# Layer 1's modulation vectors computed wholly on VectorE, in three places of a two-layer diffusion backbone

## The chip, the cores and the metric

The kernel runs on one core of a Trainium2 chip. What counts is the device time of one execution in microseconds; lower is better. The kernel before took 1163.95, 1163.52 and 1162.24 us in three runs, a median of 1163.52 us.

## The reference

Two layers, each a token-mixing part and a feed-forward part, for 256 latent tokens (modulated by `c`) and 128 context tokens (modulated by `c_ctx`), 1024 wide. Cut to what matters here:

```python
def layer(x, mod, p, latent, kc, vc):
    sh1, sc1, g1, sh2, sc2, g2 = split(mod, 6)        # six vectors of 1024
    h = layer_norm(x) * (1 + sc1) + sh1               # group A: sh1, sc1
    z = h @ p["w_in"] + p["b_in"]
    ... attention, depthwise convolution, Fourier mixing, three gated projections -> merged
    x = layer_norm(ALPHA * x + g1 * (merged @ p["w_o"]), p["ln1_g"], p["ln1_b"])   # group G: g1
    h = layer_norm(x) * (1 + sc2) + sh2               # group B: sh2, sc2
    u = dwconv3(h @ p["w_up"], ...)
    ug, uv = split(u, 2)
    x = layer_norm(ALPHA * x + g2 * ((silu(ug) * uv) @ p["w_down"]), p["ln2_g"], p["ln2_b"])  # G: g2

for l in range(2):
    mod_ctx = silu(c_ctx) @ w_mod[l] + b_mod[l]       # w_mod[l]: 1024 x 6144
    mod_lat = silu(c) @ w_mod[l] + b_mod[l]
    ...
```

So each layer needs six vectors of 1024 for each of two conditions: groups A (shift and scale ahead of the mixing), G (the gate of the mixing, index 0, and that of the feed-forward part, index 1) and B (shift and scale ahead of the feed-forward part).

## The kernel before

All weights are fp32. A product is made of three matmuls (`mm3`, L196 to L198): weight and activation are each split in a high part (`whi`, cast by ScalarE, L179) and the rest (`wlo`, a subtraction on VectorE, L180). Weights come in 1 MB tiles (`raw`, 128x2048), all loaded by `load` (L121), nearly all of them from SyncE's queue. A scheduler puts the instructions of each engine in a fixed order ahead of time; at run time each engine (and SyncE's queue of DMA issues) works its list strictly in that order, and an instruction that waits holds all behind it.

The modulation vectors are made in three ways:

- Group A of layer 0, at the start, on TensorE (`mod_first`).
- G and B of layer 0, and G and B of layer 1, on TensorE, each in the mixing part of its own layer: `mod_stream` loads `w_mod` in 256 KB pieces, eight to a step, and each step issues eight small fp32 matmuls (L217, `acc<-s,cpad`; the trace shows them as 16 records). There are eight steps to a layer. The last step of G ends in `mod_gates` (a memset on GpSimd at L268, four bias loads, an addition, four writes to the DRAM scratch `gscr`), the last of B in `mod_columns` (a copy out of PSUM on VectorE, L282; four transposes on TensorE, L286; four additions, L294).
- Group A of layer 1, on VectorE, in layer 0's feed-forward loop: `mod_rows` takes `w_modr`, the same weights stored the other way, in 512 KB tiles of 128x1024; each tile is multiplied with the broadcast rows of silu(c) and silu(c_ctx) and summed along the row (L315, SCALAR_TENSOR_TENSOR with `accum_out`, two to a tile). There are 16 tiles, hence 32 such instructions. The two broadcast rows come from the DRAM scratch `cscr`, which the setup writes at L154.

The gates are read back from `gscr` by `gate_bc`, each row broadcast to 128 partitions (512 KB a read), just ahead of the `close` that uses them: L817 multiplies the PSUM result by the gate, L818 adds the residual, L820 and L824 apply the layer norm's scale `lg` and bias `lb`, which `ln` loads bring.

In the mixing part the attention's scores and softmax come first, mixed with the taps of the depthwise convolution (L785, VectorE); then branches 1 and 2, whose products are gated on VectorE (L562) and added up on GpSimd (L563, `g<-g,g`). In the feed-forward part a loop over u = 0 to 10 makes two pairs of up-projection tiles (taps of the small convolution on ScalarE L927 and VectorE L928, L930; the gating L946 to L951) and one piece of the down projection.

Of the kernel before, what the change touches and what calls it, by code (L numbers as in the profile page):

```python
# [16 lines left out]
P = 128  # L17
D = 1024
# [59 lines left out]
class Net:  # L78
# [3 lines left out]
    def __init__(self, ctx, tc, a):  # L82
        self.tc, self.nc, self.a = tc, tc.nc, a
        self.sb = ctx.enter_context(tc.tile_pool(name="sb", bufs=1))
        self.ps = ctx.enter_context(tc.tile_pool(name="ps", bufs=1, space=bass.MemoryType.PSUM))
        self.dr = ctx.enter_context(tc.tile_pool(name="dr", bufs=1, space=bass.MemoryType.DRAM))
        self.n = 0
        self.modcol, self.bmod, self.colsets = {}, {}, {}


    def t(self, tag, shape, dtype=F32):
# [39 lines left out]
    def setup(self):  # L131
        nc, a = self.nc, self.a
        self.zeros = self.const("zeros", [P, P])
        nc.vector.memset(self.zeros, 0.0)
        self.busy(self.WARM)
        self.ident = self.const("ident", [P, P])
        make_identity(nc, self.ident)
        self.mhalf = self.const("mhalf", [P, 1])
        nc.gpsimd.memset(self.mhalf, -0.5)
        self.zero2 = self.const("zero2", [P, 2 * KD])  # L140
        nc.gpsimd.memset(self.zero2, 0.0)
        self.cpad = self.const("cpad", [P, KD, 32])
        nc.gpsimd.memset(self.cpad, 0.0)
        ct, ch = self.kk()[0:2 * KD, :], self.kk()[0:2 * KD, :]
        self.load(ct, a["c2"])
        nc.vector.tensor_scalar(ch, ct, 0.5, None, op0=ALU.mult)
        nc.scalar.activation(ct, ch, AF.Tanh)
        nc.vector.scalar_tensor_tensor(ch, ct, 1.0, ch, op0=ALU.add, op1=ALU.mult)
        pt = self.psum()
        nc.tensor.transpose(pt[:, 0:2 * KD], ch, self.ident[0:2 * KD, 0:2 * KD])  # L150
        nc.vector.tensor_copy(
            self.cpad[:, :, 0:2], pt[:, 0:2 * KD].rearrange("p (v k) -> p k v", v=2))
        self.cscr = self.dr.tile([2, D], F32, tag="cscr", name="cscr", bufs=1)
        nc.sync.dma_start(self.cscr.rearrange("v (k p) -> (v k) p", p=P), ch)  # L154
        self.gscr = self.dr.tile([DEPTH, 2, 2, D], F32, tag="gscr", name="gscr", bufs=1)
        self.xscr = self.dr.tile([3, P, D], F32, tag="xscr", name="xscr", bufs=1)

    def setup_late(self):
        nc, a = self.nc, self.a
        att = self.const("att", [P, 128 + 768])  # L160
        self.load(att, a["k_att"])
        self.rope = att[:, 0:128].rearrange("p (t s c) -> p t s c", t=2, s=2)
        self.mask = att[:, 128:896].rearrange("p (t k) -> p t k", t=2)
        self.kT = [[self.sb.tile([P, 512], F32R, tag=f"kT{v}{i}", name=f"kT{v}{i}", bufs=1) for i in range(2)]
                   for v in range(NKV)]
        self.upad = [self.const(f"upad{i}", [P, UP_W]) for i in range(2)]
        for u in self.upad:
            nc.gpsimd.memset(u, 0.0)
# [124 lines left out]
                dst = self.modcol[l][:, gi, v, ks].rearrange("p (i q) -> p i q", q=ns)  # L293
                nc.vector.tensor_tensor(dst, part, bias, op=ALU.add)  # L294

    def mod_rows(self, l, kind):

        nc, a = self.nc, self.a
        cb = [self.bcast(self.cscr[v]) for v in range(2)]
        prod = self.s4()  # L300
        w = [self.s4() for _ in range(2)]
        b0 = 3 if kind == "B" else 0
        tiles = [(j, k) for j in range(2) for k in range(KD)]
        sums = [self.sm(16) for _ in range(2)]

        def fetch(n):
            j, k = tiles[n]
            self.load(w[n % 2], a["w_modr"][l - 1, self.MODS[kind], j, k])

        fetch(0)  # L310
        fetch(1)
        yield
        for n, (j, k) in enumerate(tiles):
            for v in range(2):
                nc.vector.scalar_tensor_tensor(prod, w[n % 2], 1.0, cb[v], op0=ALU.mult, op1=ALU.mult,  # L315
                                               accum_out=sums[j][:, v * KD + k:v * KD + k + 1])
            if n + 2 < len(tiles):
                fetch(n + 2)
            if k == KD - 1:
                for v in range(2):  # L320
                    nc.vector.tensor_tensor(self.modcol[l][:, j + (2 if kind == "B" else 0), v, :],
                                            sums[j][:, v * KD:(v + 1) * KD], self.bmod[l][:, j + b0, :], op=ALU.add)
            yield

    def gate_bc(self, l, j):
        out = []
# [179 lines left out]
        self.b_out(l, 1, acc, z, bb)  # L506


    def mixing(self, l, first, hT, mods):
        nc, a = self.nc, self.a  # L510
        z = [self.s4() for _ in range(3)]
        (self.start_first if l == 0 else self.start_next)(l, first, hT, z)
# [57 lines left out]

        if l + 1 < DEPTH:
            self.columns(l + 1)
        mods = self.mod_stream(mods)

        def mod():
            next(mods, None)

        ci = conv_in()
        next(ci)
        cv = self.keys(l, z)  # L580
# [20 lines left out]
                mod()  # L601
        for i, _ in enumerate(branch(1, 0, "w_a", 4, aT, lambda: values(3))):
            next(cb, None)
            if i % 2:
                mod()
        for i, _ in enumerate(branch(2, 1, "w_c", 2, cT, lambda: [None for _ in cb])):
            if i % 2:
                mod()
        for _ in mods:
            pass  # L610
        return m_hl

    def fourier(self, f, out):
# [228 lines left out]
    TAIL = 5  # L842
    NF = 4

    def layer(self, l, first, hT, mods):
        nc, a = self.nc, self.a
        m_hl = self.mixing(l, first, hT, mods)
        gate = self.gate_bc(l, 0)
        lg, lb = self.bcast(a["ln"][l, 0]), self.bcast(a["ln"][l, 1])
        acc = [[self.psum("acc"), self.psum("acc")] for _ in range(3)]  # L850
# [53 lines left out]
            for q in range(2):  # L904
                self.split_hT(t, 4 * q, 4, h2f[t][q], h2, GAP)

        rows = self.mod_rows(l + 1, "A") if l + 1 < DEPTH else iter(())
        gT = {}
        off2 = (0, P, 2 * P + GAP)
        held = []  # L910
# [23 lines left out]
        for u in range(KF // 2):  # L934
            ws = []
            for v in range(2):
                if 2 * u + v * KF in pre:
                    ws.append([None, None])
                else:
                    ws.append(self.halves(self.col_halves(self.raw(a["w_u"][l, u, v]))))  # L940
            for h in range(2):
                i = 2 * u + h
                cg = up_tile(i, ws[0][h])
                th = self.g()
                nc.scalar.activation(th, cg, AF.Tanh)  # L945
                nc.vector.scalar_tensor_tensor(cg, th, 1.0, cg, op0=ALU.add, op1=ALU.mult)  # L946
                cv = up_tile(KF + i, ws[1][h])
                nc.vector.tensor_tensor(cg, cg, cv, op=ALU.mult)  # L948
                hi, lo = self.r(), self.r()
                nc.scalar.copy(hi, cg)  # L950
                nc.vector.tensor_tensor(lo, cg, f32(hi), op=ALU.subtract)  # L951
                gT[i] = (hi, lo)
                if u >= 2:
                    next(rows, None)
            if u >= 1:
                down(u - 1)
        down(KF // 2 - 1)
        gate = self.gate_bc(l, 1)
        lg, lb = self.bcast(a["ln"][l, 2]), self.bcast(a["ln"][l, 3])
# [45 lines left out]
    def run(self):  # L1005
        self.setup()
        xhat = [self.s4() for _ in range(3)]
        for t in range(3):
            self.load(xhat[t], self.x_src(0, t))
        self.columns(0)  # L1010
        for x in xhat:
            self.norm(x, x, D)
        mods = [[(0, "G"), (0, "B")], [(1, "G"), (1, "B")]]
        first, hT = xhat, self.new_hT(0)
        for l in range(DEPTH):
            first, hT = self.layer(l, first, hT, mods[l])


@with_exitstack
# [8 lines left out]
def layout(i):  # L1028
# [30 lines left out]
    modr = g[1:][:, :, :, [0, 1]].reshape(L - 1, D, 1, 2, KD, P).transpose(0, 2, 3, 4, 5, 1)  # L1059
    kvf = cat([w_in[:, :, C_K:C_CONV], w_in[:, :, C_F:C_G]], 2)  # L1060
    up = a["w_up"]
    out = {
# [33 lines left out]
```

## Time and profile before

| | us |
|---|---|
| median of three runs | 1163.52 |
| the profiled execution's own time | 1162.13 |
| its span, first to last instruction | 1160.3 |
| TensorE busy | 1139.3 |
| VectorE busy | 785.1 |
| ScalarE busy | 522.9 |
| GpSimd busy | 77.5 |
| granted TensorE clock, mean | 0.996 of full speed |

The engines' busy times are sums of the recorded durations; matmuls overlap one another and TensorE's idle time is given by what ended it. The chain of waits follows the execution back from its last instruction and says which engine held the end at each step. The windows give busy time in a stretch. What matters for the change is read from three stretches: layer 0's feed-forward part (about 320 to 575 us), layer 1's mixing part (about 600 to 850 us) and layer 1's feed-forward part with the end of the program (from about 885 us).

### The profile page before, as it was taken

What the parts mean: (1) busy time and instruction counts of PE and PEld (TensorE: products, weight loads), DVE (VectorE), ACT (ScalarE), POOL (GpSimd) and SP (SyncE); (2) the same over time, 40 slices, a digit from 0 to 9 for tenths busy, and PEclk for the clock granted to TensorE, in tenths of its full rate; (3) what the DMA queues carried; (4) which work ended last, traced back from release to release, by engine and by line L of the source; (5) the groups of instructions that cost most, each with busy time, mean ns of one, the idle gap of its engine ahead of it and who ended that gap; (6) DMA issues with size and microseconds to landing.
All of it is one profiled execution on the core that took longest, in us unless ns stands there. A gap on an engine that the chain in (4) does not pass through costs nothing.

```text
span 1160.3 us, 16670 instructions
## 1 busy us (share of the span) xinstructions
PE 1139.3 (98%) x6569; PEld 1019.4 (88%) x6569; DVE 785.1 (68%) x1332; ACT 522.9 (45%) x875; POOL 77.5 (7%) x91
## 2 busy tenths in 40 slices
PE   8999999999999999999999999999999999999996
PEld 6788888898999999999958978889989999999995
DVE  5579965445799976666776799444477666555667
ACT  2457743242754344444372766233447444334440
POOL 1010001121100000000021000111110000000001
PEclk9999999999999999999999999999999999999998
DMA  9764567633366663343335364783427333333411
GB/s 362 295 205 145 167 229 271 231 141 127 128 236 206 229 206 139 109 136 119 110 122 216 118 218 155 277 313 109 146 73 251 112 114 141 113 142 109 146 37 55
DMA packets 47806, 195.95 MB, mean 169 GB/s; under 512 B 5552, under 2 KB 6608, under 8 KB 32624
## 3 DMA queue, kind: packets, MB, share of 16 engines
q1 hardware_dynamic: 47296, 194.10, 47.3%
q8 instruction: 52, 0.85, 0.3%
q10 hardware_dynamic: 432, 0.79, 0.2%
q14 instruction: 26, 0.21, 0.0%
HBM read 191.41 MB, written 3.45 MB: 168 GB/s over the span
## 4 chain that ended last, share of the span: by engine, by line
PE 84%; DVE 8%; ACT 2%; DMA 2%; POOL 1%; issue 1%; SPq 0%; POOLq 0%; DVEq 0%; ACTq 0%
PE ps L196 16%; PE ps L198 16%; PE ps L197 16%; PE acc L196 9%; PE acc L197 9%; PE acc L198 9%; PE acc L217 2%; PE acc L767 1%; DVE sm L372 1%; DVE wlo L180 1%; POOL sm L376 1%; DVE s L818 1%; DVE s L828 1%; PE acc L755 1%; ACT whi L179 1%
## 5 line engine op out<-in xcount | busy, mean ns | idle before, releaser
L180 DVE TENSOR_TENSOR wlo<-raw,whi 128x1024 fp32r<-128x1024 f32 x216 | 269.1, 1247 | 236.2 <-ACT whi L179 227.2
L196 PE MATMUL ps<-hT,whi 128*128 128x386 f32 (+1 forms) x1088 | 370.3, 340 | 1.8 <-ACT g L548 1.5
L198 PE MATMUL ps<-hT,wlo 128*128 128x386 f32 (+1 forms) x1088 | 368.7, 339 | 0.0
L197 PE MATMUL ps<-hT,whi 128*128 128x386 f32 (+1 forms) x1088 | 368.4, 339 | 0.0
L179 ACT CAST whi<-raw 128x1024 fp32r<-128x1024 f32 x216 | 225.8, 1049 | 308.1 <-PE ps L197 211.4
L196 PEld LDWEIGHTS ps<-hT,whi 128*128 128x128 f32 x1088 | 205.2, 189 | 14.1 <-ACT whi L179 5.0
L197 PEld LDWEIGHTS ps<-hT,whi 128*128 128x128 f32 x1088 | 205.2, 189 | 2.7 <-issue 1.7
L198 PEld LDWEIGHTS ps<-hT,wlo 128*128 128x128 f32 x1088 | 205.3, 189 | 0.3 <-issue 0.3
L197 PE MATMUL acc<-wlo,r 128*128 128x512 f32 x360 | 142.3, 395 | 0.0
L196 PE MATMUL acc<-whi,r 128*128 128x512 f32 x360 | 142.1, 395 | 0.0
L198 PE MATMUL acc<-whi,r 128*128 128x512 f32 x360 | 141.9, 394 | 0.0
L198 PEld LDWEIGHTS acc<-whi,r 128*128 128x128 f32 x360 | 67.6, 188 | 16.2 <-DVE r L951 0.5
L196 PEld LDWEIGHTS acc<-whi,r 128*128 128x128 f32 x360 | 67.6, 188 | 14.9
L197 PEld LDWEIGHTS acc<-wlo,r 128*128 128x128 f32 x360 | 67.6, 188 | 14.4
L785 DVE SCALAR_TENSOR_TENSOR cv<-upad,cst,cv 128x399 f32<-128x399 f32 x120 | 70.1, 627 | 0.1
L376 POOL TENSOR_TENSOR sm<-sm,mhalf 128x1 f32<-128x1 f32 x21 | 23.0, 1099 | 612.4 <-DVE sm L375 611.7
L950 ACT CAST r<-g 128x386 fp32r<-128x386 f32 x44 | 22.7, 515 | 89.5 <-DVE g L948 89.5
L927 ACT ACTIVATE g<-ps,cst 128x386 f32<-128x386 f32 x84 | 56.3, 670 | 0.0
L930 DVE SCALAR_TENSOR_TENSOR g<-ps,cst,g 128x385 f32<-128x385 f32 x84 | 52.0, 619 | 2.3
L928 DVE SCALAR_TENSOR_TENSOR g<-ps,cst,g 128x385 f32<-128x385 f32 x84 | 51.6, 614 | 0.2
L563 POOL TENSOR_TENSOR g<-g,g 128x384 f32<-128x384 f32 x32 | 35.8, 1118 | 181.8 <-DVE g L562 173.3
L945 ACT ACTIVATE g<-g 128x386 f32<-128x386 f32 x44 | 23.2, 527 | 45.2 <-DVE g L930 45.2
(185 smaller groups left out, 1353.0 us busy)
## 6 DMA issues: line engine op xcount, KB each, us to landing
raw<-w_u SPq DMA_DIRECT2D x44, 1024.0 KB, 4.8
s<-w_mod SPq DMA_DIRECT2D x128, 256.0 KB, 4.4
raw<-w_g SPq DMA_DIRECT2D x24, 1024.0 KB, 7.8
raw<-w_d SPq DMA_DIRECT2D x22, 1024.0 KB, 4.9
raw<-w_mod SPq DMA_DIRECT2D x8, 1024.0 KB, 9.5
raw<-w_o SPq DMA_DIRECT2D x8, 1024.0 KB, 4.8
s<-w_modr SPq DMA_DIRECT2D x16, 512.0 KB, 4.2
s<-w_z SPq DMA_DIRECT2D x8, 512.0 KB, 9.7
```

The costliest lines, as they stand in the source:

```text
L179: self.nc.scalar.copy(hi, raw)
L180: self.nc.vector.tensor_tensor(lo, raw, f32(hi), op=ALU.subtract)
L196: mm(ps, lh, rh, start=first, stop=False)
L197: mm(ps, lh, rl, start=False, stop=False)
L198: mm(ps, ll, rh, start=False, stop=last)
L217: self.nc.tensor.matmul(ps[32 * i:32 * i + 32, 0:n], self.cpad[:, k, :], src[k, i], start=ks[0] == 0 and k == ks[-1], stop=ks[-1] == KD - ...
L376: nc.gpsimd.tensor_tensor(mv[:, 3:4], mv[:, 2:3], self.mhalf, op=ALU.pow)
L563: nc.gpsimd.tensor_tensor(merged[m], merged[m], gt, op=ALU.add)
L785: nc.vector.scalar_tensor_tensor(c, u[:, i:i + CV_W], w, c, op0=ALU.mult, op1=ALU.add)
L927: nc.scalar.activation(c, ps, AF.Identity, bias=cols["ffn_b"][:, i:i + 1], scale=w[1])
L928: nc.vector.scalar_tensor_tensor(c[:, 1:NPAD], ps[:, 0:NPAD - 1], w[0], c[:, 1:NPAD], op0=ALU.mult, op1=ALU.add)
L930: nc.vector.scalar_tensor_tensor(c[:, 0:NPAD - 1], ps[:, 1:NPAD], w[2], c[:, 0:NPAD - 1], op0=ALU.mult, op1=ALU.add)
```

## The change

- `mod_stream` is used for layer 0 alone. Layer 1's eight steps on TensorE, with the memset, the bias loads, the `gscr` writes, the copy and the transposes behind them, are gone.
- `mod_rows` now takes a list of units. Layer 0's feed-forward loop computes A and B of layer 1: 32 tiles, 64 of the multiply-and-sum instructions (now L318), from u = 1 on. Layer 1's branches 1 (from its fifth tile) and 2 compute gate (1, G, 0): 8 tiles, 16 instructions. Layer 1's feed-forward loop computes gate (1, G, 1): 8 tiles, 16 instructions. `paced` spreads the steps over the slots of each place. Each of the three places loads the two broadcast rows of `cscr` for itself.
- A gate's sums lie in a 128x16 column tile. `gate_rows` transposes it on TensorE (L338), copies it out of PSUM on ScalarE (L340) and writes it to `gscr` by one DMA (L341): at the end of the mixing part, and in the feed-forward part after the last step of the loop.
- The write of `cscr` moves from the setup to `setup_late`, and `w_modr` holds both layers and all groups.

```diff
@@ setup, setup_late
         self.cscr = self.dr.tile([2, D], F32, tag="cscr", name="cscr", bufs=1)
-        nc.sync.dma_start(self.cscr.rearrange("v (k p) -> (v k) p", p=P), ch)
+        self.silu = ch
...
     def setup_late(self):
+        nc.sync.dma_start(self.cscr.rearrange("v (k p) -> (v k) p", p=P), self.silu)
@@ mod_rows(self, units)
+        tiles = [(n, k) for n in range(len(units)) for k in range(KD)]
+        sums = [self.sm(16) for _ in units]
...
+        for i, (n, k) in enumerate(tiles):
             for v in range(2):
+                nc.vector.scalar_tensor_tensor(prod, w[i % 2], 1.0, cb[v], op0=ALU.mult, op1=ALU.mult,
+                                               accum_out=sums[n][:, v * KD + k:v * KD + k + 1])
+            if i + 2 < len(tiles):
+                fetch(i + 2)
...
+                if kind == "G":
+                    self.gate_sums.append((l, j, sums[n]))
             yield
+    def gate_rows(self, tag):
+        nc = self.nc
+        for l, j, cols in self.gate_sums:
+            pt = self.psum(tag)[0:2 * KD, 0:P]
+            nc.tensor.transpose(pt, cols, self.ident)
+            row = self.kk()[0:2 * KD, :]
+            nc.scalar.copy(row, pt)
+            nc.sync.dma_start(self.gscr[l, j].rearrange("v (k p) -> (v k) p", p=P), row)
+        self.gate_sums = []
+    def paced(self, units, slots):
+        steps = self.mod_rows(units) if units else iter(())
+        need, done = len(units) * KD + 1, [0, 0]
+        def step():
+            done[0] += 1
+            while done[1] * slots < need * done[0]:
+                done[1] += 1
+                next(steps, None)
+        return step
@@ mixing
-        mods = self.mod_stream(mods)
+        mods = self.mod_stream(mods) if mods else iter(())
+        step_rows = self.paced(rows, 10)
...
+            if i >= 4:
+                step_rows()                 # in branch 1
...
+            step_rows()                     # in branch 2
...
+        self.gate_rows("acc")
@@ layer
-        rows = self.mod_rows(l + 1, "A") if l + 1 < DEPTH else iter(())
+        step_rows = self.paced(rows, 17 if len(rows) > 1 else 9)
...
-                if u >= 2:
-                    next(rows, None)
+                if u >= 1:
+                    step_rows()
             if u >= 1:
                 down(u - 1)
+            if u == KF // 2 - 1:
+                self.gate_rows("ps")
@@ run
-        mods = [[(0, "G"), (0, "B")], [(1, "G"), (1, "B")]]
+        mods = [[(0, "G"), (0, "B")], []]
+        mix_rows = [[], [(1, "G", 0)]]
+        ffn_rows = [[(1, "A", 0), (1, "A", 1), (1, "B", 0), (1, "B", 1)], [(1, "G", 1)]]
```

How this stands on the engines, at three places. On TensorE in layer 1's branches, where the last of the eight steps stood between the products of branch 1 (`acc_7332`) and the next weights (`ps_7386`), before:

```order
L198 MATMUL acc_7332<-r_6848,wlo_7142 128x384
L217 MATMUL acc_6921<-s_7251,cpad 32x512
L217 MATMUL acc_6921<-s_7249,cpad 32x512
L217 MATMUL acc_6921<-s_7247,cpad 32x512
L217 MATMUL acc_6921<-s_7245,cpad 32x512
L217 MATMUL acc_6921<-s_7243,cpad 32x512
L217 MATMUL acc_6921<-s_7241,cpad 32x512
L217 MATMUL acc_6921<-s_7239,cpad 32x512
L217 MATMUL acc_6921<-s_7237,cpad 32x512
L196 MATMUL ps_7386<-hT_5332,whi_7368 128x384
```

Now no L217 stands anywhere in layer 1, and a branch's products are followed directly by the next weights. On VectorE in the same stretch stands, in its place, the work of the first gate, after (L594 is the gating that was L562, L182 the `wlo` that was L180):

```order
L182 TENSOR_TENSOR wlo_7226<-raw_7223,whi_7225 128x1024
L594 SCALAR_TENSOR_TENSOR g_7103<-g_7103,acc_7105 128x384
L182 TENSOR_TENSOR wlo_7230<-raw_7223,whi_7229 128x1024
L318 SCALAR_TENSOR_TENSOR s_7072,sm_7075<-s_7073,s_7068 128x1024
L318 SCALAR_TENSOR_TENSOR s_7072,sm_7075<-s_7073,s_7070 128x1024
L318 SCALAR_TENSOR_TENSOR s_7072,sm_7075<-s_7074,s_7068 128x1024
L182 TENSOR_TENSOR wlo_7236<-raw_7233,whi_7235 128x1024
L594 SCALAR_TENSOR_TENSOR g_7158<-g_7158,acc_7160 128x384
L318 SCALAR_TENSOR_TENSOR s_7072,sm_7075<-s_7074,s_7070 128x1024
```

One to three of the new instructions stand between two weight splits. The end of the feed-forward loop of layer 1, on SyncE's queue, after (`w_d` are the last down-projection weights; L862 are the outputs):

```order
L122 DMA raw_10058<-w_d 128x2048
L122 DMA raw_10073<-w_d 128x2048
L341 DMA gscr<-kk_10070 16x128
L122 DMA s_10083<-gscr 128x1024
L122 DMA s_10085<-gscr 128x1024
L122 DMA s_10087<-ln 128x1024
L122 DMA s_10089<-ln 128x1024
L862 DMA o_xs<-s_10151 128x512
```

The gate's write and, behind it, the two gate reads and the two `ln` loads are now the last loads of the program; before, the reads of `gscr` and `ln` for this part stood at its beginning. What the write waits for stands on TensorE, after, between the last up-projection tile (`ps_10024`) and the tail of the down projection (`acc_8267`):

```order
L199 MATMUL ps_10024<-hT_7786,whi_9922 128x386
L200 MATMUL ps_10024<-hT_7785,wlo_9923 128x386
L338 MATMUL ps_10068<-ident,sm_8195 16x128
L198 MATMUL acc_8267<-whi_9884,r_9676 128x512
L199 MATMUL acc_8267<-wlo_9885,r_9676 128x512
```

The sums `sm_8195` that it transposes are finished earlier; the transpose is simply listed this late.

## Rows read from the trace of the kernel before

**Rows 1.** The page, parts 1 and 4: busy time and instructions; chain by engine.

```profile
PE 1139.3 (98%) x6569; PEld 1019.4 (88%) x6569; DVE 785.1 (68%) x1332; ACT 522.9 (45%) x875; POOL 77.5 (7%) x91
PE 84%; DVE 8%; ACT 2%; DMA 2%; POOL 1%; issue 1%; SPq 0%; POOLq 0%; DVEq 0%; ACTq 0%
```

**Rows 2.** Windows of line L217 alone: length, TensorE busy (records), PEld; clock; DMA.

```profile
671.00:721.00 50.00, 6.16 (x48) 1.02 (x48) 1.00 0.58 194
...
748.00:800.00 52.00, 5.77 (x48) 1.25 (x48) 1.00 0.71 264
```

**Rows 3.** TensorE's timeline, layer 1's branches: start, duration, line, tiles, idle before.

```profile
770.26 0.34 PE L198 MATMUL acc<-r,wlo 128*128 128x384 f32 x1
770.52 1.92 PE L217 MATMUL acc<-s,cpad 128*32 128x512 f32 x16
...
772.66 0.34 PE L197 MATMUL ps<-hT,whi 128*128 128x384 f32 x1
772.83 0.34 PE L198 MATMUL ps<-hT,wlo 128*128 128x384 f32 x1
```

**Rows 4.** TensorE's timeline around the transposes L286.

```profile
788.01 0.33 PE L198 MATMUL ps<-hT,wlo 128*128 128x384 f32 x1
788.73 0.66 PE L286 MATMUL acc<-ident,s 128*128 128x128 f32 x4 [0.39 <-DVE s L282]
...
789.40 0.34 PE L197 MATMUL ps<-hT,whi 128*128 128x384 f32 x1
```

**Rows 5.** VectorE by lines, 318 to 416 us: count, busy, mean ns, idle before.

```profile
L315 DVE SCALAR_TENSOR_TENSOR s<-s,s 128x1024 f32<-128x1024 f32 x32 | 38.9, 1216 | 0.8 <-DMA s<-w_modr 0.7
```

**Rows 6.** Windows, layer 0's feed-forward loop: length; PE, PEld, DVE, ACT, POOL; clock; DMA.

```profile
318.00:416.00 98.00, 97.67 (x538) 91.97 (x537) 93.96 (x152) 44.33 (x65) 0.00 (x0) 1.00 0.64 222
416.00:514.00 98.00, 98.00 (x513) 91.82 (x512) 60.09 (x84) 40.40 (x55) 0.00 (x0) 1.00 0.42 144
514.00:570.00 56.00, 56.00 (x297) 52.81 (x296) 36.53 (x50) 24.08 (x33) 0.00 (x0) 1.00 0.34 115
```

**Rows 7.** Windows of layer 1's mixing part, columns as in rows 6.

```profile
671.00:721.00 50.00, 50.00 (x324) 42.03 (x323) 47.22 (x108) 32.76 (x82) 0.00 (x0) 1.00 0.58 194
748.00:800.00 52.00, 51.61 (x314) 46.26 (x314) 25.26 (x41) 17.54 (x24) 8.64 (x10) 1.00 0.71 264
```

**Rows 8.** The page, part 5: the convolution's taps, both layers.

```profile
L785 DVE SCALAR_TENSOR_TENSOR cv<-upad,cst,cv 128x399 f32<-128x399 f32 x120 | 70.1, 627 | 0.1
```

**Rows 9.** Timelines of VectorE (two rows) and GpSimd (one), 769 to 773 us.

```profile
769.43 1.23 DVE L180 TENSOR_TENSOR wlo<-raw,whi 128x1024 fp32r<-128x1024 f32 x1 [4.49 <-ACT whi L179]
771.53 1.89 DVE L180 TENSOR_TENSOR wlo<-raw,whi 128x1024 fp32r<-128x1024 f32 x1 [0.28 <-ACT whi L179]
...
771.34 1.01 POOL L563 TENSOR_TENSOR g<-g,g 128x384 f32<-128x384 f32 x1 [5.30 <-DVE g L562]
```

**Rows 10.** Timelines of TensorE, ScalarE and VectorE at the program's end.

```profile
1129.47 0.40 PE L196 MATMUL acc<-whi,r 128*128 128x512 f32 x1
...
1130.45 0.67 ACT L927 ACTIVATE g<-ps,cst 128x386 f32<-128x386 f32 x1
...
1135.32 0.69 DVE L817 TENSOR_TENSOR s<-acc,s 128x512 f32<-128x512 f32 x1 [0.58 <-PE acc L198]
...
1150.66 0.69 DVE L817 TENSOR_TENSOR s<-acc,s 128x512 f32<-128x512 f32 x1 [0.26 <-PE acc L198]
```

**Rows 11.** A window from the first `close` to the last, columns as in rows 6.

```profile
1135.32:1156.75 21.43, 15.30 (x66) 12.02 (x64) 20.31 (x33) 0.00 (x0) 4.50 (x3) 0.93 0.14 50
```

**Rows 12.** Tile gscr: microseconds from a read's issue to its landing.

```profile
DMA to landing us min/median/max: 4.1/6.5/7.3
```

**Rows 13.** DMA issues: count, KB each, median us to landing.

```profile
o_xs<-s SPq DMA_DIRECT2D x2, 256.0 KB, 2.1
```

**Rows 14.** The chain of waits, first 18 us: start, length, what.

```profile
5.53 0.33 SPq L154
...
7.79 9.84 DMA s<-w_z
```

More of the change, by code (lines that the diff above doesn't have):

```diff
@@ L294, in mod_columns, with mod_rows @@
                 nc.vector.tensor_tensor(dst, part, bias, op=ALU.add)
-    def mod_rows(self, l, kind):
-        nc, a = self.nc, self.a
+    def mod_rows(self, units):
+        nc = self.nc
         cb = [self.bcast(self.cscr[v]) for v in range(2)]
@@ L301, in mod_rows, with fetch @@
         w = [self.s4() for _ in range(2)]
[L302 to L308, printed above, removed]
+        tiles = [(n, k) for n in range(len(units)) for k in range(KD)]
+        sums = [self.sm(16) for _ in units]
+        def fetch(i):
+            n, k = tiles[i]
+            l, kind, j = units[n]
+            self.load(w[i % 2], self.a["w_modr"][l, self.MODS[kind], j, k])
         fetch(0)
@@ L312, in mod_rows @@
         yield
-        for n, (j, k) in enumerate(tiles):
+        for i, (n, k) in enumerate(tiles):
             for v in range(2):
[L315 to L318, printed above, removed]
+                nc.vector.scalar_tensor_tensor(prod, w[i % 2], 1.0, cb[v], op0=ALU.mult, op1=ALU.mult,
+                                               accum_out=sums[n][:, v * KD + k:v * KD + k + 1])
+            if i + 2 < len(tiles):
+                fetch(i + 2)
             if k == KD - 1:
+                l, kind, j = units[n]
+                bias = self.bmod[l][:, {"A": (0, 1), "B": (3, 4), "G": (2, 5)}[kind][j], :]
+                dst = sums[n] if kind == "G" else self.modcol[l][:, j + (2 if kind == "B" else 0)]
                 for v in range(2):
-                    nc.vector.tensor_tensor(self.modcol[l][:, j + (2 if kind == "B" else 0), v, :],
-                                            sums[j][:, v * KD:(v + 1) * KD], self.bmod[l][:, j + b0, :], op=ALU.add)
+                    d = dst[:, v * KD:(v + 1) * KD] if kind == "G" else dst[:, v, :]
+                    nc.vector.tensor_tensor(d, sums[n][:, v * KD:(v + 1) * KD], bias, op=ALU.add)
+                if kind == "G":
+                    self.gate_sums.append((l, j, sums[n]))
             yield
+    def gate_rows(self, tag):
+        nc = self.nc
+        for l, j, cols in self.gate_sums:
[4 more added lines that the diff above has]
+            nc.sync.dma_start(self.gscr[l, j].rearrange("v (k p) -> (v k) p", p=P), row)
+        self.gate_sums = []
+    def paced(self, units, slots):
[7 more added lines that the diff above has]
+        return step
     def gate_bc(self, l, j):
@@ L506, in start_next, with mixing @@
         self.b_out(l, 1, acc, z, bb)
-    def mixing(self, l, first, hT, mods):
+    def mixing(self, l, first, hT, mods, rows):
         nc, a = self.nc, self.a
@@ L843, with layer @@
     NF = 4
-    def layer(self, l, first, hT, mods):
+    def layer(self, l, first, hT, mods, mix_rows, rows):
         nc, a = self.nc, self.a
-        m_hl = self.mixing(l, first, hT, mods)
+        m_hl = self.mixing(l, first, hT, mods, mix_rows)
         gate = self.gate_bc(l, 0)
@@ L1012, in run @@
             self.norm(x, x, D)
-        mods = [[(0, "G"), (0, "B")], [(1, "G"), (1, "B")]]
+        mods = [[(0, "G"), (0, "B")], []]
+        mix_rows = [[], [(1, "G", 0)]]
+        ffn_rows = [[(1, "A", 0), (1, "A", 1), (1, "B", 0), (1, "B", 1)], [(1, "G", 1)]]
         first, hT = xhat, self.new_hT(0)
         for l in range(DEPTH):
-            first, hT = self.layer(l, first, hT, mods[l])
+            first, hT = self.layer(l, first, hT, mods[l], mix_rows[l], ffn_rows[l])
 @with_exitstack
@@ L1058, in layout @@
     mod = np.stack([g[:, :, :, [0, 1]], g[:, :, :, [3, 4]], g[:, :, :, [2, 5]]], 1)
-    modr = g[1:][:, :, :, [0, 1]].reshape(L - 1, D, 1, 2, KD, P).transpose(0, 2, 3, 4, 5, 1)
+    modr = mod.reshape(L, 3, D, 2, KD, P).transpose(0, 1, 3, 4, 5, 2)
     kvf = cat([w_in[:, :, C_K:C_CONV], w_in[:, :, C_F:C_G]], 2)
```

## The prediction

> **What bounds the kernel now.** I read the page first, then the windows of three stretches, then timelines. TensorE is busy 1139.3 of 1160.3 us and carries 84% of the chain, VectorE is busy 785.1 us [rows 1]. Over the whole, TensorE sets the time and VectorE has room. By stretch the room is unequal. In layer 0's feed-forward loop VectorE is busy 94.0 of 98 us while it does the sums for group A, and 60.1 of the next 98 [rows 6]; TensorE is busy 97.7 and 98.0 in the two. In layer 1's attention stretch VectorE is busy 47.2 of 50 us, in the branches 25.3 of 52 [rows 7]. At the end the roles change: VectorE is busy 20.3 of 21.4 us while TensorE is at 15.3 [rows 11]. So work taken from TensorE counts fully only where VectorE keeps up, and what comes late at the end counts fully at once.
>
> **What goes from TensorE: -17.4 us.** Each of layer 1's eight steps shows as 16 records [rows 3], three steps (48 records) lie between 671 and 721 us and three between 748 and 800 [rows 2]. The records overlap, so I price a step by what it displaces. Between the matmul ahead of it, at 770.26, and the second one behind it, at 772.66, lie 2.40 us, where neighbours stand 0.17 apart [rows 3]: two pitches are 0.35, so a step costs 2.05, eight cost 16.4. The transposes L286 go too: from 788.01 to 789.40 are 1.39, less two pitches 1.04 [rows 4], of which 0.39 was a wait for VectorE's copy. The copy and its four additions leave VectorE. The memset leaves GpSimd, where nothing on the path waited for it. Nothing else ran under these steps that TensorE would now have to wait for, except VectorE's own work, below.
>
> **Start: -0.7 us.** SyncE held its queue for the `cscr` write, which was issued at 5.53; the loads behind it, among them the `w_z` piece that lands 9.84 us after 7.79 and sets the first matmul, come behind that [rows 14]. Without the write these issues move up by its 0.33 and by the time that the queue was held for it. The loads are then limited by the transfers of one another, so I take 0.7, twice the 0.33, between 0 and 1.4. The write itself stands behind the early weights now; its first reader comes in layer 0's feed-forward loop.
>
> **Layer 0's feed-forward loop: +1.0 us.** It had 32 multiply-and-sum instructions and gets 64, spread to twice the length. One takes 1.216 us [rows 5]. The second 98 us window, 60.1 busy, gets 32 of them with 38.9 us: 99.0 of 98. The first stays near 94.0. The third has 19.5 us idle [rows 6], so an overflow can be taken up there, but only as far as the fixed order lets TensorE's next weights (`wlo`, on VectorE) go ahead. TensorE lost 0.33 in the first window under nearly that load. Bounds: 0, and 5.2 if VectorE gets no further than in the first window, 96% busy, and nothing is absorbed (99.0 / 0.959 = 103.2). I take 1.0, nearer to the 0.33 of the window that was loaded. The DMA traffic doubles in the second window, to about the 222 GB/s which the first one moves [rows 6] with one wait of 0.7 us [rows 5]. The 16 sums in layer 1's loop meet a VectorE as free as in that second window, and cost nothing.
>
> **Layer 1's attention stretch: +1.3 us.** Three steps [rows 2], 6.15 us, leave TensorE between 671 and 721, but VectorE has only 2.8 us idle there [rows 7]. TensorE can gain more only if VectorE has less to do before the same matmuls. The new order puts about ten of the convolution's taps later at one place, ten times 0.627 [rows 8], or 6.3 us; by that all 6.15 could be gained, without it 3.4 are lost. Since taps are put off only in the middle of the stretch, I take 1.3, bounds 0 and 3.4.
>
> **Layer 1's branches: +1.0 us, and +0.3.** The 16 sums of the first gate stand here: 19.5 us. VectorE's idle 26.7 of 52 [rows 7] shrink by what TensorE no longer spends, three steps [rows 2] and the transposes, 7.2, to 19.5, plus about 1 us for the copy and additions that go. This is full to the brim. Further, VectorE's `wlo` took 1.89 at 771.53 beside a GpSimd addition that had begun at 771.34, and 1.23 without one [rows 9]: 0.66 held, until about that addition's end. GpSimd has ten instructions in this window [rows 7], so at most 6.6 more if each holds one. Ends: 0 and 5.6 (6.6 less the 1 us); holds occurred already, and TensorE works some way behind VectorE here, so I take 1.0. The gate's transpose adds 0.3, twice a quarter of the 0.65 that the four L286 cost without their wait; its result is needed only in the `close`, behind most of the output projection.
>
> The Trainium skill, "SBUF — State Buffer", section "Who interferes with whom", says that a VectorE instruction with two SBUF inputs and a GpSimd one that reads SBUF exclude each other for the whole instruction. The trace agrees, with the 0.66. By that rule each sum here, with two SBUF inputs, is open to such a hold, and the term would be at its upper end, 5.6, and the forecast 1156.4.
>
> **The end: +2.8 us.** The gate of the last part now goes through a chain that starts late: transpose behind the last up tile (1129.47), ScalarE's copy behind its last tile's L927, which ends at 1131.12 [rows 10], the write, then the two reads. Before, these reads were issued at the beginning of this part. The copy costs at most as much as that L927, 0.67: 1131.8. The nearest row of a write is 2.1, for 256 KB [rows 13]; I take it: 1133.9. The second read is issued about 0.35 later and lands in at best 4.1, median 6.5, at most 7.3 [rows 12]; the queues are nearly empty at the end (50 GB/s, rows 11), so 4.1: 1138.4. The first L817 started at 1135.32 [rows 10], so it is 3.1 late, and as VectorE is busy nearly all the way to the end, only the 0.26 for which it waits for TensorE at 1150.66 [rows 10] gives back: 2.8. Lower end: a read as short as the 2.1, 0.7 in all. Upper end: a write as long as the shortest read, 4.1, and a read of 7.3, which makes 8.0. The `ln` loads behind the gates are due a few us after the first L817 and should land in time.
>
> The Trainium skill, "DMA: Bandwidth & Descriptors", section "Anatomy of one DMA — SWDGE (gpsimd) path", fits a DMA as 2.0 us plus its bytes at 436 GB/s. For the write and both reads that makes, as an estimate, 2.0 + 2.0 + 2.4, so the first `close` would be 2.9 late, the term 2.6, and the sum 0.2 lower; these DMAs come from SyncE and no run here shows that fit.
>
> **Sum.** -17.4 - 0.7 + 1.0 + 1.3 + 1.0 + 0.3 + 2.8 = -11.7. The profiled execution's own time was 1162.13 (span 1160.3 and 1.8 around it), so 1150.4; the median of the three runs lies 1.4 above it: 1163.5 - 11.7 = 1151.8 us.
>
> **Rivals.**
> - VectorE is the bound in all three stretches. For it: 94.0 of 98 and 47.2 of 50 busy. Against it: TensorE lost only 0.33 us in the loaded window. Terms at their upper ends, 5.2, 3.4 and 5.6, in place of 3.3 in all: 10.9 more, 1162.7, no change; half of it 1157.2. Chance 0.15.
> - The chain at the end is slow: 8.0 in place of 2.8, 1157.0. For it: the median of 6.5 for the same reads. Against it: those landed beside weight loads. Chance 0.12.
> - All removed time is gained, and VectorE's lateness is absorbed: -18.1 + 0.3 + 0.7 = -17.1, 1146.4. Chance 0.14.
> - Slower: in layer 0's loop the weights for the sums come late tile by tile. The loop has two buffers, SyncE's queue issues in order, and VectorE cannot do its `wlo` past a sum that waits. If every one of 32 tiles costs the 0.7 seen once [rows 5], 22.4 us are lost, of which the first window's 4.0 idle absorb a part: 18.4 in place of 1.0 gives 1169.2. It decides from 0.5 per tile on (16.0 - 4.0 = 12). Against it: of 16 tiles one waited. Chance 0.05.
> - The change does nothing: TensorE's gaps move to later waits, 1163.5. Against it: the pieces around every step are TensorE's own. Chance 0.04.
>
> **How the numbers follow.** My forecast has 0.50, about 1149 to 1155. With the cases the range 1146.3 to 1158 holds some 0.8: it takes in the slow end of the chain, half of VectorE's case, and nearly the full gain. About 0.2%, 2.3 us, can be told from no change. Faster: 0.50 + 0.14 + 0.12 + 0.13 = 0.89; same: 0.04 + 0.02 = 0.06; slower 0.05.
>
> **What would show it.** No L217 and no L286 after 600 us, and the stretch from 671 to 849 shorter by about 15. TensorE idle in 671 to 721 with VectorE as releaser would show the attention term; TensorE waiting for `wlo` in layer 0's loop, or VectorE for `w_modr`, the loop's. First L817 of the last `close` released by the DMA from `gscr` 3 us after TensorE was done is the end's term; released by TensorE it is wrong. The prediction is wrong if layer 0's loop grows by more than 4 us or the last gate's read lands before TensorE's result.

## The result, and the profile after

The changed kernel takes 1147.22 us (median of four, 1144.76 to 1148.19), 16.5 us less than the kernel before, which now stands at 1163.74. The ratio is 0.9856, with a 95% interval of 0.9839 to 0.9873. The forecast was 1151.8, with a range of 1146.3 to 1158: right in direction and inside the range, with 4.6 us too little gain. Of the kernels below, one execution of only G took 2873.1 us and stands in no ratio.

The page of the changed kernel, parts 1 and 4, answers to [rows 1]:

```profile
PE 1124.1 (98%) x6439; PEld 1016.2 (89%) x6439; DVE 850.9 (74%) x1462; ACT 521.8 (46%) x877; POOL 84.5 (7%) x90
PE 84%; DVE 8%; ACT 2%; DMA 2%; issue 1%; POOL 1%; SPq 0%; POOLq 0%; DVEq 0%; ACTq 0%
```

TensorE has 15.2 us and 130 records less, VectorE 65.8 us more, and the share of the chain is the same: TensorE stays the bound. To see where the time went, I laid the start of the same instructions of both timelines beside one another: the weight splits `wlo` on VectorE, whose order is the same in all kernels here, and the last normalisation. At 267.6, 590.8, 654.4, 825.0 and 1127.4 us of the kernel before the changed kernel stands 0.27, 0.41, 0.41, 16.10 and 15.92 us earlier, and at the last normalisation 14.64. So nearly everything is gained in layer 1's mixing part, nothing that can be told is lost in either feed-forward part (0.14 less and 0.18 more), and 1.3 us are given back at the end.

Windows of layer 0's feed-forward loop after, which answer to [rows 6]:

```profile
318.00:416.00 98.00, 97.83 (x539) 92.25 (x538) 94.03 (x152) 44.13 (x64) 0.00 (x0) 1.00 0.64 220
416.00:514.00 98.00, 98.00 (x513) 91.72 (x512) 93.59 (x151) 40.14 (x54) 0.00 (x0) 1.00 0.66 221
514.00:570.00 56.00, 56.00 (x295) 52.74 (x294) 36.01 (x49) 24.41 (x34) 0.00 (x0) 1.00 0.38 133
```

The second window now looks like the first: VectorE at 93.6 of 98, the DMA traffic up from 144 to 221 GB/s, and TensorE still busy in all 98. The end of the program, on ScalarE, SyncE and VectorE (three timelines), answers to [rows 10]:

```profile
1114.52 0.67 ACT L964 ACTIVATE g<-ps,cst 128x386 f32<-128x386 f32 x1
1115.09 0.24 ACT L340 COPY kk<-ps 16x128 f32<-16x128 f32 x1
...
1115.35 0.33 SPq L341 DMA_DIRECT2D gscr<-kk  x1
1116.72 0.81 SPq L122 DMA_DIRECT2D s<-gscr  x2
...
1118.23 0.56 DVE L988 TENSOR_TENSOR r<-g,r 128x386 fp32r<-128x386 f32 x1 [0.58 <-ACT r L987]
1122.14 1.29 DVE L854 TENSOR_TENSOR s<-acc,s 128x512 f32<-128x512 f32 x2 [3.34 <-DMA s<-gscr]
...
1134.82 0.69 DVE L854 TENSOR_TENSOR s<-acc,s 128x512 f32<-128x512 f32 x1
...
1140.70 1.42 DVE L861 SCALAR_TENSOR_TENSOR s<-s,sm,s 128x512 f32<-128x512 f32 x2 [0.44 <-POOL sm L408]
```

The copy is at 1115.09, the write behind it, the reads are issued 1.37 after the write, and VectorE sits idle for 3.34 us until a read lands. In the kernel before, VectorE had these rows, with the first multiplication (1135.32, [rows 10]) between them:

```profile
1134.18 0.56 DVE L951 TENSOR_TENSOR r<-g,r 128x386 fp32r<-128x386 f32 x1 [0.58 <-ACT r L950]
...
1155.34 1.41 DVE L824 SCALAR_TENSOR_TENSOR s<-s,sm,s 128x512 f32<-128x512 f32 x2 [0.44 <-POOL sm L376]
```

There 1.14 us lay between L951 and the first multiplication by the gate, now 3.91 lie between L988 and L854: it is 2.8 late.

### The profile page after: what moved, and what is told of

Same layout as the page of the kernel before. It is cut to its first block, busy times and chain, and to the rows that moved or that the text cites. A ratio compares the mean times of both kernels' runs of the same rounds, so it can differ in the third digit from the quotient of the medians.

```text
span 1145.2 us, 16511 instructions
## 1 busy us (share of the span) xinstructions
PE 1124.1 (98%) x6439; PEld 1016.2 (89%) x6439; DVE 850.9 (74%) x1462; ACT 521.8 (46%) x877; POOL 84.5 (7%) x90
## 4 chain that ended last, share of the span: by engine, by line
PE 84%; DVE 8%; ACT 2%; DMA 2%; issue 1%; POOL 1%; SPq 0%; POOLq 0%; DVEq 0%; ACTq 0%
PE ps L198 17%; PE ps L200 16%; PE ps L199 16%; PE acc L198 9%; PE acc L199 9%; PE acc L200 9%; PE acc L804 1%; PE acc L219 1%; DVE sm L404 1%; DVE s L855 1%; POOL sm L408 1%; DMA raw<-w_mod 1%; PE acc L792 1%; DVE wlo L182 1%; DMA s<-w_modr 1%
## 5 line engine op out<-in xcount | busy, mean ns | idle before, releaser
L182 DVE TENSOR_TENSOR wlo<-raw,whi 128x1024 fp32r<-128x1024 f32 x216 | 267.8, 1241 | 164.9 <-ACT whi L181 164.9
L318 DVE SCALAR_TENSOR_TENSOR s<-s,s 128x1024 f32<-128x1024 f32 x96 | 119.3, 1243 | 3.7 <-DMA s<-w_modr 3.3
L200 PEld LDWEIGHTS acc<-whi,r 128*128 128x128 f32 x360 | 67.6, 188 | 15.8 <-DVE r L988 0.3
L595 POOL TENSOR_TENSOR g<-g,g 128x384 f32<-128x384 f32 x32 | 41.3, 1292 | 250.8 <-DVE g L594 243.1
```

Of the source, the lines that this page charges most:

```text
L182: self.nc.vector.tensor_tensor(lo, raw, f32(hi), op=ALU.subtract)
L200: mm(ps, ll, rh, start=False, stop=last)
L318: nc.vector.scalar_tensor_tensor(prod, w[i % 2], 1.0, cb[v], op0=ALU.mult, op1=ALU.mult, accum_out=sums[n][:, v * KD + k:v * KD + k + 1])
L595: nc.gpsimd.tensor_tensor(merged[m], merged[m], gt, op=ALU.add)
```

## The experiments

For each kernel the table gives, from such pairs of timelines, how much longer (+) or shorter (-) each stretch of the profiled execution is than in the kernel before, and the timed medians' difference to the kernel before on the same chip (a star: the kernel of that row was executed once).

| kernel | start to 267.6 | layer 0's feed-forward part | layer 1's mixing part | layer 1's feed-forward part | end | timed |
|---|---|---|---|---|---|---|
| changed kernel | -0.27 | -0.14 | -15.69 | +0.18 | +1.28 | -16.5 |
| early last gate | -0.41 | +0.55 | -15.67 | +0.28 | +0.02 | -16.6 |
| only B moved | -1.16 | -0.53 | -9.16 | +0.01 | +0.02 | -11.6 |
| only G moved | -1.77 | -0.30 | -8.59 | +0.64 | +1.31 | -9.8 |
| second gate in layer 0 | -0.97 | +2.76 | -15.63 | +0.10 | 0.00 | -15.8 |
| all in layer 0 | -1.06 | +22.00 | -15.85 | 0.00 | +0.04 | +4.3* |
| fewer taps, changed | +0.05 | -0.14 | -15.70 | +0.15 | +1.30 | -15.2* |
| fewer taps, before | +1.86 | -0.08 | +0.24 | -0.02 | +0.02 | +1.5* |
| taps later | -2.77 | -0.30 | -14.21 | +0.24 | +0.02 | -16.8 |
| steps late | +1.58 | -0.16 | +11.54 | -0.78 | +0.01 | +11.3* |
| before, late `cscr` | +1.28 | -0.19 | +0.02 | -0.01 | +0.03 | -2.8 |
| changed, early `cscr` | +0.33 | -0.13 | -15.61 | +0.09 | +1.31 | -14.6 |

The same edit gives the same stretch to about 0.1 us in the mixing part and at the end, and to about 0.6 either way in layer 0's feed-forward part; the start varies by up to 4 us between kernels that write `cscr` late (-2.77 to +1.28).

**The last gate early.** Does the late chain cost what the end lost?

```diff
-            if u == KF // 2 - 1:
+            if u == 6:
                 self.gate_rows("ps")
```

> The changed kernel with one line different: the last gate's transpose, copy and write are emitted behind u = 6 of layer 1's feed-forward loop in place of behind u = 10, so the write and the two gate reads stand before the last weight loads. Theory (late chain): in the changed kernel the first multiplication by the gate stood 3.3 us idle for the gate's read, and the last output came 1.2 us later against TensorE's end than before the change; with the early chain the first multiplication follows TensorE's result (under 0.8 us of idle), the stretch from TensorE's last up tile to the last output is that of the kernel before, 25.9 us from first small matmul of the tail to last normalisation, and the time is 1.2 us below the changed kernel, about 1146.0. Rival (the delay is the reads of scale and bias or VectorE's own work): the stretch stays as long as in the changed kernel, 27.1 us, time 1147.2. Rival (all 2.8 us of the lateness count): 1144.4.

Timed 1146.67 (ratio 0.9858, 0.9841 to 0.9874), which cannot be told from the changed kernel by time. The stretch can: the end is +0.02 in place of +1.28. VectorE's timeline of this kernel:

```profile
1118.93 0.56 DVE L988 TENSOR_TENSOR r<-g,r 128x386 fp32r<-128x386 f32 x1 [0.58 <-ACT r L987]
1120.09 0.69 DVE L854 TENSOR_TENSOR s<-acc,s 128x512 f32<-128x512 f32 x1 [0.59 <-PE acc L200]
...
1140.12 1.41 DVE L861 SCALAR_TENSOR_TENSOR s<-s,sm,s 128x512 f32<-128x512 f32 x2 [0.44 <-POOL sm L408]
```

TensorE releases the first multiplication again, and from there to the last normalisation are 20.03 us, as before (20.02). In the changed kernel they were 18.56: 2.8 us late at the beginning, VectorE does the same work 1.5 us faster, since the scheduler now lists it in pairs that don't depend on each other (x2 in the rows after, two of 0.69 in 1.29), which start 0.60 apart. So the late chain is the cause, and its price in the stretch is 1.3. The second rival, all 2.8, is refuted.

**One half and the other.**

```diff
-        mods = [[(0, "G"), (0, "B")], []]
-        mix_rows = [[], [(1, "G", 0)]]
-        ffn_rows = [[(1, "A", 0), (1, "A", 1), (1, "B", 0), (1, "B", 1)], [(1, "G", 1)]]
+        mods = [[(0, "G"), (0, "B")], [(1, "G")]]                                          # only B
+        mix_rows = [[], []]
+        ffn_rows = [[(1, "A", 0), (1, "A", 1), (1, "B", 0), (1, "B", 1)], []]
...
+        mods = [[(0, "G"), (0, "B")], [(1, "B")]]                                          # only G
+        mix_rows = [[], [(1, "G", 0)]]
+        ffn_rows = [[(1, "A", 0), (1, "A", 1)], [(1, "G", 1)]]
```

> Half of the change: group B of layer 1 goes to VectorE in layer 0's feed-forward loop (64 sums there), its gates G stay on TensorE in layer 1's mixing part (four steps) with the old writes. Theory (each step is worth 2.05 us, the loop hides the doubled sums, the end's delay belongs to the gate): TensorE loses four steps and the transposes, 8.2 + 1.0 = 9.2, the start gives 0.3, the end is that of the kernel before: -9.5 and up to 1 of loss, time 1154.2 to 1155.2. Rival (doubling the sums in layer 0's loop costs what the branches then gave back): layer 0's feed-forward part over 1 us longer than the 246.9 of before, time above 1156.

> The other half: the two gates of layer 1 go to VectorE (one in layer 1's branches, one in its feed-forward loop), group B stays on TensorE in layer 1's mixing part (four steps, its transposes) and layer 0's loop has the 32 sums of before. Theory: four steps leave, 8.2, the start gives 0.3, the end loses 1.2 as in the changed kernel, the attention stretch up to 0.8: -6.5 to -7.3, time 1156.4 to 1157.2. Rival (the 16 sums in the branches, held by GpSimd's additions, slow TensorE): TensorE idle for the weight splits between 750 and 800 us, and the time above 1159.

Only B: 1151.69 (0.9903, 0.9888 to 0.9917), 2.5 better than expected; the mixing part is 9.16 shorter, as the 9.2 said to a tenth. Only G: 1153.47 (0.9917, 0.9901 to 0.9934), 2.9 better than expected; mixing part -8.59, end +1.31. In both some 2 to 3 us of the time lie outside the stretches that I had priced, which sent me back to the start. And the two halves make 17.75 in the mixing part, the whole only 15.69. In each half the four steps that stay take the first four places, in the attention stretch, so what is gone are the last four. The loss of 1.7 thus belongs to taking the first four away, and not to the sums in the branches, which the second half has too.

**How much more layer 0's loop takes.**

```diff
-        ffn_rows = [[(1, "A", 0), (1, "A", 1), (1, "B", 0), (1, "B", 1)], [(1, "G", 1)]]
+        ffn_rows = [[(1, "A", 0), (1, "A", 1), (1, "B", 0), (1, "B", 1), (1, "G", 1)], []]                 # second gate
+        ffn_rows = [[(1, "A", 0), (1, "A", 1), (1, "B", 0), (1, "B", 1), (1, "G", 0), (1, "G", 1)], []]    # all
+        mix_rows = [[], []]                                                                                # all
```

> The changed kernel with the second gate (1, G, 1) moved to layer 0's feed-forward loop: 80 sums there, none in layer 1's loop, and the gate's chain is done 500 us before its use. Theory (VectorE gives room until it is full: 190.6 us busy of 252 with 32 sums before, 48 more at 1.2 make 248): layer 0's part grows by 0 to 2 us over the 246.8 of the changed kernel, the end gains 1.2, so the time lies between 1146.0 and 1148.0. Rival (the loop is already bound by VectorE in the changed kernel): each of the 16 added sums adds its full 1.15, 18 us, time 1164.

> All six units of layer 1's modulation in layer 0's feed-forward loop, 96 sums. VectorE's work there is then 190.6 - 32 x 1.2 + 96 x 1.2 = 267 us in a part of 252. Theory (TensorE's loss is what VectorE is over full, and it was 2.7 with 80 sums): layer 0's part, from the last close of the mixing part to the first close of the feed-forward part, grows by 15 us or more against before; the other stretches as in the run with the second gate moved; time about 1159 to 1163. Rival (the fixed order hides it, sums wait in the 56 us without them): growth under 5, time below 1150.

With 80 sums 1147.53 (0.9867, 0.9852 to 0.9881): layer 0's part +2.76, a little over the expected 2, the end 0.00. With 96 sums 1166.93 in one execution: +22.0, slower than before. The waits of TensorE there, first with 80 sums, then with 96 (total us, times, longest):

```profile
PE ps L198 <- DVE g L967: 1.5, 3, 1.0
PE acc L199 <- DVE wlo L182: 1.0, 1, 1.0
```

```profile
PE acc L199 <- DVE wlo L182: 12.4, 4, 5.0
PE ps L198 <- DVE g L967: 1.8, 3, 0.9
```

So TensorE waits for VectorE from somewhere above 64 sums on, and each of the last 16 costs 1.2 us. That this comes to a sum's full duration is chance, since the waits are only 15.3 of the 22.0. In this kernel the granted clock is lower too, 0.97 and 0.96 in the windows with the two waits of some 5 us (1.00 in all three windows with 80 sums):

```profile
318.00:416.00 98.00, 91.24 (x482) 84.23 (x481) 94.21 (x154) 39.80 (x57) 0.00 (x0) 0.97 0.64 221
...
514.00:592.00 78.00, 73.50 (x374) 68.18 (x374) 69.47 (x107) 30.10 (x43) 0.00 (x0) 0.96 0.62 223
```

By estimate (0.03 of 98 and 0.04 of 78) that is up to 6 us more. The rival of the full VectorE is real, and the change stops just short of it.

**What the first four steps lacked.** The theory was the prediction's: without them VectorE is the bound in the attention stretch.

```diff
         for i in range(CONV_K):                  # both kernels: fewer taps in layer 1
+        for i in range(CONV_K - 8 * l):
...
-            next(cb, None)                       # branch 0, on top of the early last gate: taps later
+            if l == 0 or i % 2:
+                next(cb, None)
```

> The changed kernel without 8 of the 31 taps of layer 1's depthwise convolution (16 instructions of 0.63 us on VectorE are left out, so the output is not the reference's). In the changed kernel layer 1's mixing part got 15.7 us shorter, 1.7 less than the 17.4 that its eight steps and the transposes cost, and with only the last four steps gone it got all of 9.2. Theory (VectorE is the bound in the attention stretch once the first four steps are gone): with 10 us less to do there, the stretch gains the missing 1.7, the mixing part is at least 17.0 shorter than before. Rival (TensorE waits for copies and exponentials of ScalarE, or for the order): the mixing part stays 15.7 shorter, within 0.4.

> The kernel before, with the same 8 taps of layer 1 left out: the control. Theory (VectorE was just not the bound there): the mixing part of layer 1 is as long as in the kernel before, within 0.5 us. Rival (VectorE held TensorE there already): it gets shorter by 1 us or more, and a gain by the taps in the changed kernel would then say nothing on the change.

> The changed kernel with the early last gate, and in layer 1 the convolution's taps emitted half as fast during branch 0 (the attention stretch), the rest later. Nothing is left out. Theory (VectorE is the bound in the attention stretch): up to 1.7 us more than with the early gate alone, mixing part 16.0 to 17.4 shorter than before, time about 1145.0, if the taps do not then arrive late at branch 2. Rival (they do, or VectorE is full in the branches with the 16 sums): the mixing part is less than 15.7 shorter, time 1146.7 or above.

With 8 taps fewer (the last ones, so the output is not the reference's) the changed kernel's mixing part is -15.70, as with all of them, and the control +0.24. The theory gets no support, but it is not refuted either: the taps left out all stood behind 707 us, and from 655 to 705 VectorE stayed as busy, 47.59 of 50 us (47.62 in the changed kernel). With the taps moved back it is busy 47.69 there, and the mixing part is -14.21, 1.5 worse, of which 0.7 is a wait of TensorE for the convolution's normalisation; that its time is near the others' all the same (1145.78 us, 0.9856, 0.9835 to 0.9877) goes with a short start in the profile (-2.77).

What the timelines show is where the gain is missing. Stretches from one set of scores (L726, now L763) to the next hold the same 66 matmuls before and after, apart from one step each:

| step, and its stretch in the kernel before | before | after | gained |
|---|---|---|---|
| first, in two halves, 665.12 to 678.41 | 13.29 | 11.35 | 1.94 |
| second, whole, 684.60 to 696.97 | 12.37 | 10.47 | 1.90 |
| third, in two halves, 703.17 to 714.91 | 11.74 | 10.89 | 0.85 |

With 6.5 for the first four (15.69 less 9.16), 1.8 remain for the fourth. So of the missing 1.7, 1.2 belong to the third step. TensorE's timeline there in the kernel before, then in the changed kernel:

```profile
704.96 1.06 PE L217 MATMUL acc<-s,cpad 128*32 128x512 f32 x8
705.96 0.88 PE L755 MATMUL acc<-ident,g 128*128 128x128 f32 x6
706.67 0.27 PE L756 MATMUL acc<-ident,kk 128*128 128x128 f32 x1
706.87 1.06 PE L217 MATMUL acc<-s,cpad 128*32 128x512 f32 x8
707.87 1.08 PE L767 MATMUL acc<-s,s 128*64 128x256 f32 x8
708.78 0.60 PE L767 MATMUL acc<-s,col 128*64 128x256 f32 x4
709.21 0.39 PE L770 MATMUL acc<-s,s 128*64 128x128 f32 x4
```

```profile
701.79 0.27 PE L793 MATMUL acc<-ident,kk 128*128 128x128 f32 x1
701.99 1.27 PE L804 MATMUL acc<-s,s 128*64 128x256 f32 x8
703.20 0.44 PE L198 MATMUL ps<-hT,whi 128*128 128x384 f32 x1
703.48 0.33 PE L199 MATMUL ps<-hT,whi 128*128 128x384 f32 x1
703.74 0.65 PE L804 MATMUL acc<-s,col 128*64 128x256 f32 x2
704.32 0.44 PE L200 MATMUL ps<-hT,wlo 128*128 128x384 f32 x1
704.68 0.43 PE L804 MATMUL acc<-s,col 128*64 128x256 f32 x1
```

Behind the transposes of the probabilities (L756, now L793) the products with the values (L767 and L770, now L804 and L807) need copies by ScalarE and VectorE. Before, the two halves of the step stood in front of the second transposes and of the products, which then ran in one piece. Now the products begin earlier, and matmuls of the next weights stand between them in TensorE's list. From each start to the next the products take 1.66 us before and 2.57 after, and the weights' matmuls of the stretch 5.38 and 5.85, so the step was partly filler there. Over the whole part the products take 8.29 us in the kernel before and 9.31 in the changed one, and 9.51 and 9.20 in the two with the taps fewer or later. With the taps later the three stretches gain 1.97, 1.58 and 1.39, so the loss also hangs on the order of VectorE's work; whether a freer VectorE would end it, no run shows.

**The steps away from the attention.** The kernel before, to see the same without any of the change:

```diff
-            if i % 2:
+            if i % 2 and l == 0:                 # branch 0
                 mod()
```

> The kernel before with one line different: in layer 1 no step of the modulation is taken in branch 0, so that all eight stand in branches 1 and 2, away from the attention's scores and values. Theory (filler: in the attention stretch half-steps of 1.0 us stand between the transposes of the probabilities and the products that wait for their copies, and cost less than 2.05 a step): moved to where TensorE never waits, the first four cost their full 8.2 in place of 6.5, so layer 1's mixing part is 1.2 to 2.2 us longer than in the kernel before. Rival (a step costs the same everywhere and the missing 1.7 us come from something that the change adds, the sums or their loads): the mixing part is as long as before, within 0.4.

A miss in size: 1174.26, and the mixing part 11.5 longer. Waits of the last steps for their weights, and of the transposes for VectorE's copy, are 7.9 of it:

```profile
PE acc L217 <- DMA s<-w_mod: 4.3, 3, 2.0
PE acc L286 <- DVE s L282: 3.6, 1, 3.6
```

But the first part can be read. Where four steps fewer have run than in the kernel before (from 749 to 779 us), this kernel is 6.6 us ahead of where it stood at 654, not 8.2; the three stretches of the table gain 1.97, 1.90 and 0.85, and the products with the values take 9.30. So the four steps were worth 6.6 also where VectorE has no sum to do and no weight goes another way: the missing 1.7 come from taking the steps out of their places, not from the sums or their loads.

**The start.**

```diff
-        nc.sync.dma_start(self.cscr..., ch)      # the kernel before: from setup to setup_late
...
+        nc.sync.dma_start(self.cscr..., self.silu)
```

> The kernel before with the cscr write moved behind the early weight loads, and nothing else of the change. In the profiles so far the first close of layer 0 starts at 282.2, 284.0 and 283.7 us in three kernels with the early write and between 279.4 and 282.2 (mean 281.1) in eight with the late one. Theory (the held queue costs about 2 us at the start): the first close at 279.5 to 282.2, the time 1 to 3 us below the kernel before. Rival (the first loads are bound by each other's transfers, the differences are those of single executions): time within 0.7 of the kernel before.

> The changed kernel with the cscr write put back to its early place. Theory (the held queue costs about 2 us): the first close at 282 to 284, the time 1 to 3 us above the changed kernel, 1148.2 to 1150.2. Rival (no effect of the queue): first close near 281, time near 1147.2.

The kernel before with the late write: 1160.44 (median of 11), ratio 0.9979 (0.9970 to 0.9988), so 1.4 to 3.5 us faster, 2.4 by the middle. The changed kernel with the early write: 1148.59, ratio 0.9882 (0.9866 to 0.9898) where the changed kernel has 0.9856 (0.9839 to 0.9873), so 3.0 us slower by the ratios, 1.9 by the medians, with intervals that overlap. The first pair is clear of the noise and the second agrees: the write's place is a good 2 us of the whole gain. Single profiles don't show it. In that first kernel's, of its slowest execution, the first `close` came at 283.4 us, later than expected, and the start was 1.28 longer; but the granted clock from 12 to 25 us is 0.61 in it and 0.87 in the kernel before. Among timed executions with the same mean clock, 0.994, the late write has 1160.70 and 1161.41 us, the early one 1162.65 to 1164.29. What the profiles show is the queue, here SyncE's timeline of the kernel before, then of the changed kernel:

```profile
5.53 0.33 SPq L154 DMA_DIRECT2D cscr<-kk  x1
5.90 0.42 SPq L121 DMA_DIRECT2D s<-par  x1
6.37 0.91 SPq L121 DMA_DIRECT2D raw<-w_mod  x2
```

```profile
2.60 0.43 SPq L122 DMA_DIRECT2D s<-par  x1
3.07 0.94 SPq L122 DMA_DIRECT2D raw<-w_mod  x2
```

## Why the prediction was right, point by point

- **The steps, -17.4.** Right for the last four and the transposes (-9.16 measured for 9.2). The first four were worth 6.5 in place of 8.2, and 1.2 of the difference is the third step's. I had one step priced, in the branches, and used it for all eight, though two of the first four stood in halves between other work.
- **Attention, +1.3.** The size was near (1.7), the reason is not borne out, so the size was luck. I read a limit from VectorE's 47.2 of 50, but the sign that I had named, TensorE idle there with VectorE as releaser, does not appear: its one wait from 655 to 850 us is 0.7 for ScalarE, as before. The loss sits mainly in one place, behind transposes, and comes again without any sum. A part of VectorE in it is not excluded: the order of its taps shifts the loss, and no kernel here made VectorE freer in that stretch.
- **Layer 0's loop, +1.0.** Measured -0.5 to +0.6 in the kernels with 64 sums, so no loss that can be told. The window of before that was already loaded had said so; that VectorE then has nothing left is shown by 80 and 96 sums.
- **Branches, +1.0 and +0.3.** With the sums in the branches the mixing part is 15.6 to 15.7 shorter, without them (all in layer 0) 15.85: they and the gate's transpose cost 0.2. The holds that I priced occurred (16 x 0.155 = 2.5 us in the sums alone, below), but VectorE's lateness never reached TensorE. So the rule of the Trainium skill, "SBUF — State Buffer", section "Who interferes with whom", is the mechanism that the trace shows (last section), but the 5.6 that the prediction worked out by it is not the cost.
- **The end, +2.8.** Mechanism and lateness as forecast (2.8 late at the first multiplication), price 1.3: I took VectorE's 20.3 busy of 21.4 for full, while 1.5 of it could be made up.
- **The start, -0.7.** Mis-sized: about -2.4 by the timed pair of the kernel before. The loads behind the write are issued 3.3 us earlier (3.07 for 6.37), and I took twice the length of one issue.

With the measured terms, mixing part, feed-forward parts, end and start, it is -15.7 + 0.0 + 1.3 - 2.4 = -16.8, for -16.5 measured. The forecast had -14.8, 1.0, 2.8 and -0.7 for these four: each was off towards too little gain, by 0.9 to 1.7, so no error hid another. The rival with everything gained (1146.4) came near for a reason of its own: the start made up for what attention and end lost.

## What to carry to other kernels

Price removed work at each place where it stands, from one fixed point of the order to the next with the same matmuls between: a piece between a transpose and the matmul that needs its copy can be partly filler (0.85 of 2.05 here), and need not be (1.94 in a like place). A busy share says that an engine can be the bound, not that it is; adding to its work does, as in layer 0's loop. An edit that is meant to lighten an engine must be seen to do so in the very stretch. And a DMA issue that waits for data ahead of the first weight loads holds the whole queue: move it behind them, and expect to see that in repeated times rather than in one profile.

## What the runs showed of the hardware that was not expected

In the branches VectorE's sums and GpSimd's additions shut each other out in turn. VectorE's and GpSimd's timelines of the changed kernel:

```profile
755.75 1.21 DVE L182 TENSOR_TENSOR wlo<-raw,whi 128x1024 fp32r<-128x1024 f32 x1
756.89 2.03 DVE L318 SCALAR_TENSOR_TENSOR s<-s,s 128x1024 f32<-128x1024 f32 x1
...
755.91 1.93 POOL L595 TENSOR_TENSOR g<-g,g 128x384 f32<-128x384 f32 x1 [5.79 <-DVE g L594]
```

The addition at 755.91 waits for the split that began at 755.75 and takes 1.93 in place of 1.01 [rows 9]; the sum behind the split waits for the addition and takes 2.03. From 730 to 790 us the 16 sums take 1371 ns on average, against 1216 [rows 5], and nine additions 1524. In layer 0's loop, where GpSimd does nothing, TensorE lost nothing that can be told at a VectorE load of 96% (94.03 of 98).
